# Tiles for the conditioning dot products asked for by POOL instead of SP, and other landing times in the plan of a two-layer gated trunk

## The chip, the core and the metric

The kernel runs on one core of one Trainium2 chip. The core has a tensor engine (PE, with PEld for its weight loads), a vector engine (DVE), a scalar engine (ACT), GpSimd (POOL) and SyncE (SP), which only issues transfers. Each engine takes its instructions in one fixed order; a DMA is issued by one of the engines (here SP or ACT), after the semaphores that it waits for, and runs beside them on the core's 16 DMA engines. The metric is the time of one execution in microseconds, the median of several; each comparison is with the kernel before.

## What is computed

Two layers over a residual stream of 512 tokens and 1024 features, float32. Cut to what matters:

```python
def hybrid_layer(x, c_silu, ...):
    mod = c_silu @ w_ada + b_ada
    shift, scale, gate = jnp.split(mod, 3, axis=-1)
    u = rms_norm(x, norm_g) * (1 + scale[:, None]) + shift[:, None]
    z = u @ w_in                      # queries, keys, values, gates of all mixers
    ...
    ya = dsa_attention(...) * jax.nn.silu(ag)      # mixer A: indexer, top-k, softmax
    yb = swa_sinks_attention(...) * jax.nn.silu(bg) # mixer B: window of 128, sinks
    yc = stick_breaking_attention(...) * jax.nn.silu(cg)  # mixer C
    merged = (jax.nn.sigmoid(ma) * (ya @ w_br_a) + jax.nn.sigmoid(mb) * (yb @ w_br_b)
              + jax.nn.sigmoid(mc) * (yc @ w_br_c))
    return x + gate[:, None] * (merged @ w_out)
```

The line `mod = ...` is the conditioning: 3072 dot products of length 1024 a layer. `c` is one vector, so there is no matrix to multiply with, and the kernel does these products on DVE.

## The kernel before

**Work and stages.** Features lie on partitions, tokens along the free axis, so a tile is 128 x 512. Each float32 weight tile is split into a high and a low part (`whi`, `wlo`), each activation too (`uh`, `ul`), and TensorE adds up three products of the parts. A layer goes through a first phase (seven column groups, accumulated over the features as they become ready), a value phase, a long body, and the output phase. In the body the mixers C, B and A follow one another, each in four steps of two heads, while the remaining columns of `w_in` and the branch matrices are multiplied in between. TensorE has such weight tiles to work on all through the body. The program's name for the tiles of `w_in` is in_w_t, in_w_v and in_w_first, for the branches in_w_br_a, in_w_br_b and in_w_br_c, for the output in_w_o.

**Weights on their way.** `Chunks` (line 728 ff.) takes all weight tiles in the order of use. `load` asks for a tile in one of four buffers `wstage`, by a DMA on SP; `do_split` makes `whi` (a cast, on ACT, DVE or POOL) and `wlo` (a subtraction, on DVE or POOL) out of it, four buffers of each. A sequence entry with the flag `is_raw` is not split: it is a tile for the dot products. `ada_g` gives such tiles of in_w_gt (the gate, 16 a layer, 32 in all) and `ada_ss` those of in_w_ss (shift and scale of layer 1, 32 tiles, asked for in the body of layer 0 only; layer 0's own shift and scale come through other buffers, `Y`, before). `dot` multiplies such a tile in place by the conditioning vector (`csr`) on DVE, with the sum in one instruction, and after every second tile adds the bias into `mods`. The raw tiles use the same four `wstage` buffers as the weights, in the order of the sequence. Layer 0's gate is first needed in the output phase, in_w_ss in the first phase of layer 1.

**Rotary shuffles and transposes.** `rope_evac` turns queries and keys: it copies the product into `zs`, and four DMAs on SP bring rows of `zs` into `m2` (m in the profile, 64 KB each). `softmax_tr32` transposes attention weights by 32 x 32 blocks on DVE and by 16 DMAs from `X` to `U` (or `V5`), issued by SP or ACT. TensorE's next queries and keys (`Q`, `KH`) wait for the first, the products with the values for the second.

**The order.** Nothing of the order is written by hand. `Recorder` records all instructions with their possible engines, a price for each (`price`), and their tiles; `order` runs `forward` five times, a list scheduler that plays the engines in time: each engine takes, of what it may do, what can start first, and among these the one with the earliest latest start (`latest`) of the round before. The best of the five orders is written out, and the chip's engines follow it, each its own list, with semaphores between them. The plan's times thus set the order on each engine, the engine of each cast and subtraction, and the buffer of each tile; the chip's own times set when things happen. For a DMA the plan books the issuing engine (`price`, "dma_start": 0.35 us on SP for a load from memory, 1.0 us on POOL) and gives a landing time (line 524 ff.), with a single channel, `dma_free`, on which transfers follow one another; `lag` is the size over 385 GB/s, in us: 0.68 for 256 KB, 0.48 for 182 KB, 0.21 for 80 KB, 0.17 for 64 KB. SP's time in the plan also stops when eight transfers are under way (`LANES`); transfers of all issuing engines count there.

Of the kernel before, what the change touches and what calls it, by code (L numbers as in the profile page):

```python
# [281 lines left out]
class Recorder:  # L282
# [149 lines left out]
    def forward(self):  # L432
        E = {e: {"free": 0.0, "port": 0.0, "mode": None, "ready": {}, "pend": []} for e in self.real}
        dma_free, lanes = 0.0, []
# [12 lines left out]
        def offer(x):  # L447
            if x.left == 0 and x.bound == 0:
                for e in x.alts:
                    heapq.heappush(E[e]["pend"], (max(x.est, x.soft.get(e, 0.0)), x.i))  # L450

        def give(c):
            while c.given < len(c.tiles) and c.free:
                t = c.tiles[c.given]
                c.given += 1
                if not t.users:
                    continue
                at, slot = heapq.heappop(c.free)
                t.slot, t.before, c.held[slot] = slot, c.held.get(slot), t
                for x in waiting[id(t)]:  # L460
                    x.est = max(x.est, at)
                    x.bound -= 1
                    offer(x)
# [7 lines left out]
        while len(out) < len(self.list):  # L471
            best = None
            for name, e in E.items():
                free, port, pend, ready = e["free"], e["port"], e["pend"], e["ready"]
                while pend and pend[0][0] <= free + 1e-9:
                    i = heapq.heappop(pend)[1]
                    ready[i] = self.list[i]
                mine = None
                for i in list(ready):
                    x = ready[i]  # L480
                    if x.taken:
                        del ready[i]
                        continue
                    y = x.alts[name]
                    at = max(free, port) if y.port else free
                    if len(x.alts) > 1 and self.elsewhere(x, name, at, E):
                        continue
                    key = (at, x.prio, i)
                    if mine is None or key < mine:
                        mine = key  # L490
                if mine is None or mine[0] > free + 1e-9:
                    while pend and self.list[pend[0][1]].taken:
                        heapq.heappop(pend)
                    if pend:
                        est, i = pend[0]
                        x = self.list[i]
                        at = max(est, port) if x.alts[name].port else est
                        key = (at, x.prio, i)
                        if (mine is None or key < mine) and not (len(x.alts) > 1 and self.elsewhere(x, name, at, E)):
                            mine = key  # L500
                        elif mine is None:
                            mine = None
                if mine is not None:
                    asked = max(free, self.list[mine[2]].est, self.list[mine[2]].soft.get(name, 0.0))
                    if best is None or (mine[0], asked, mine) < best[:3]:
                        best = (mine[0], asked, mine, name)
            assert best is not None, "no instruction may go"
            (at, _, i), name = best[2:]
            e, x = E[name], self.list[i]
            y = x.alts[name]  # L510
            x.taken, x.engine = True, name
            e["ready"].pop(i, None)
            hold = y.cost
            if name == "PE":
                if e["mode"] is not None and y.mode != e["mode"]:
                    hold += self.ENTER[y.mode]
                e["mode"] = y.mode
            x.start, x.hold = at, hold
            e["free"] = at + hold
            if y.port:  # L520
                E["POOL"]["port"] = at + y.lag + self.CROSS if name == "DVE" else at + hold
                E["DVE"]["port"] = at + y.lag - self.TOPORT
            if y.mode == "dma":
                if not x.writes:
                    x.end = at + 2.1
                else:
                    x.end = dma_free = max(at + (2.1 if at < 20.0 else 2.2 if y.lag < 0.22 else 3.0), dma_free) + y.lag * (1.2 if dma_free < 5.5 else 1.0)
                lanes.append(x.end)
                if name == "SP" and len(lanes) >= self.LANES:
                    e["free"] = max(e["free"], lanes[-self.LANES])  # L530
            else:
                x.end = at + y.lag + (hold - y.cost)
            out.append(x)
            for s in x.succs:
                s.est = max(s.est, x.end + self.between(x, s))
                s.left -= 1
                offer(s)
            for s in x.apart:
                for o in s.alts:
                    if o != name:  # L540
                        s.soft[o] = max(s.soft.get(o, 0.0), x.end + self.NEXT)
                s.left -= 1
                offer(s)
            for t in x.tiles:
                t.users -= 1
                t.done = max(t.done, x.end + self.CROSS)
                if t.users == 0:
                    heapq.heappush(t.pool.free, (t.done, t.slot))
                    give(t.pool)
# [99 lines left out]
def trunk(ctx, tc, xT, vecs, w_ss, w_gt, w_first, w_t, w_v, w_br, w_o, rope, consts, out):  # L649
# [8 lines left out]
    PE, ACT, DVE, POOL, SP = (rec.engine(e) for e in ("PE", "ACT", "DVE", "POOL", "SP"))  # L658
# [69 lines left out]
    class Chunks:  # L728
# [8 lines left out]
        def load(self, upto):  # L737
            while self.nload < min(upto + 1, len(self.seq)):
                i = self.nload
                if i >= 4 and i - 4 not in self.used:  # L740
                    break
                src, is_raw = self.seq[i][:2]
                n = src.shape[1]
                t = rec.tile("wstage", [P, S], F32)
                SP.dma_start(t[:, :n], src)
                self.raw[i] = (t, n)
                self.nload += 1

# [808 lines left out]
    def out_phase(l):  # L1557
# [57 lines left out]
        for d in range(KT - 2):  # L1615
            def fn(*ws, d=d):
                z, xr = zbank(), load(d)
                mms(d, ws, z, FULL)
                update(d, z, xr, FULL)
                save(d)  # L1620
            yield op(5200, fn, (w_o[l, d, 0], False), (w_o[l, d, 1], False))

        def tail(*ws):
            z, xr = [zbank(), zbank()], [load(6), load(7)]
            parts = HALVES if l + 1 < L else (slice(0, 256), slice(256, S))
            for cs_ in parts:
                for i in range(2):
                    mms(6 + i, ws[2 * i:2 * i + 2], z[i], cs_)
                    update(6 + i, z[i], xr[i], cs_)
                if cs_.start and l + 1 == L:  # L1630
                    last(parts[0])
                after(cs_)
            if l + 1 == L:
                last(parts[1])
            save(6)
            save(7)
            st["x"] = st["xn"]
            if l + 1 < L:
                st["xold"] = st["xsave"]
# [176 lines left out]
```

## Time and profile before

| | |
|---|---|
| median of 3 runs | 1138.33 us (1137.66 to 1138.64) |
| profiled execution | 1136.31 us |
| its span, first to last instruction | 1134.2 us |
| mean granted TensorE clock | 0.998 |
| TensorE's idle time in the span | 17.9 us |
| body of layer 0 / of layer 1, about | 108 to 570 us / 664 to 1122 us |
| mean rate of all DMA | 141 GB/s |

The profiled execution is 2.0 us below the median of the others. Matmul ends are modelled, so TensorE's busy time says that work was queued, not that it ran at its peak; its idle entries are real waits. In the page, L621 is the line of the helper that writes out all recorded instructions, so instructions are told apart by the tiles that they write and read (out<-in), not by their line. An engine's name with a q (SPq) is its sequencer, where DMAs are issued.

### The profile page before, as it was taken

Reading aid. Unit: us, or ns where it says so; the run is one execution under the profiler, and the core shown is the slowest. Engines: PE = TensorE matmul, PEld = TensorE weight load, DVE = VectorE, ACT = ScalarE, POOL = GpSimd, SP = SyncE. Lnnn points to the kernel's source line nnn. Section 1 sums busy time; section 2 is a strip of 40 time slices with the busy share of each in tenths; the row PEclk is TensorE's granted clock in tenths of the full one; section 3 lists DMA queues with packets and bytes.
Section 4 is the critical chain, followed back from the end, with each engine's and each line's share of the span. In section 5 each row is a group of like instructions: output and inputs, shape, how many; then the busy total and the mean of one; then the engine's idle time right before and its main releaser. Section 6 shows DMA issues by size and latency. Waiting matters only on the chain.

```text
span 1134.2 us, 17655 instructions
## 1 busy us (share of the span) xinstructions
PE 1116.3 (98%) x5579; PEld 926.8 (82%) x5579; DVE 900.4 (79%) x1966; ACT 615.8 (54%) x1298; POOL 254.0 (22%) x340
## 2 busy tenths in 40 slices
PE   8999999999999999999999999999999999999997
PEld 6899877788878787788898988777888878877886
DVE  7865999999989896677475479999998898666544
ACT  6644765863556563444365357757436466444343
POOL 1110344632113220010011004555421222101101
PEclk9999999999999999999999999999999999999999
DMA  9644334354465566455634342253545445524342
GB/s 341 240 123 129 94 94 127 107 146 152 125 170 154 160 199 179 134 151 177 183 111 111 101 137 84 76 157 105 156 131 145 143 140 149 150 83 148 94 130 102
DMA packets 94301, 159.86 MB, mean 141 GB/s; under 512 B 14592, under 2 KB 29184, under 8 KB 94208
## 3 DMA queue, kind: packets, MB, share of 16 engines
q1 hardware_dynamic: 86096, 146.25, 43.7%
q10 hardware_dynamic: 8112, 12.49, 3.9%
q8 instruction: 44, 0.72, 0.3%
q14 instruction: 49, 0.40, 0.1%
HBM read 125.39 MB, written 4.19 MB: 114 GB/s over the span
## 4 chain that ended last, share of the span: by engine, by line
PE 87%; DVE 4%; DMA 3%; POOL 2%; ACT 1%; issue 1%; SPq 1%; DVEq 0%; POOLq 0%; ACTq 0%
PE ps_z L621 68%; PE ps_s L621 15%; PE ps_s L619 3%; SPq L621 1%; PE ps_z L619 1%; DVE X L621 1%; DMA Y<-in_w_ss 1%; DVE wlo L621 1%; POOL wlo L621 1%; DMA m<-zs 1%; DMA U<-X 1%; POOL Q L621 1%; DMA wstage<-in_w_br_c 0%; DVE m L621 0%; DVE t L621 0%
## 5 line engine op out<-in xcount | busy, mean ns | idle before, releaser
L621 PE MATMUL ps_z<-uh,whi 128*128 128x512 f32 (+1 forms) x905 | 353.9, 392 | 2.1 <-ACT KH L621 1.9
L621 PE MATMUL ps_z<-ul,whi 128*128 128x512 f32 (+1 forms) x905 | 351.5, 389 | 0.0
L621 PE MATMUL ps_z<-uh,wlo 128*128 128x512 f32 (+1 forms) x905 | 351.1, 388 | 0.0
L621 DVE TENSOR_TENSOR wlo<-wstage,whi 128x512 fp32r<-128x512 f32 (+2 forms) x315 | 213.4, 680 | 118.5 <-ACT whi L621 99.4
L621 ACT CAST whi<-wstage 128x512 fp32r<-128x512 f32 (+2 forms) x226 | 133.8, 594 | 237.3 <-PE ps_z L621 142.3
L621 PEld LDWEIGHTS ps_z<-uh,whi 128*128 128x128 f32 x905 | 169.8, 188 | 38.4 <-ACT KH L621 2.3
L621 PEld LDWEIGHTS ps_z<-uh,wlo 128*128 128x128 f32 x905 | 169.8, 188 | 34.5 <-issue 0.2
L621 PEld LDWEIGHTS ps_z<-ul,whi 128*128 128x128 f32 x905 | 169.9, 188 | 33.1 <-issue 0.5
L621 POOL CAST whi<-wstage 128x512 fp32r<-128x512 f32 (+2 forms) x109 | 67.5, 619 | 489.2 <-PE ps_z L621 280.5
L621 PE MATMUL ps_z<-Y,whi 128*128 128x512 f32 x384 | 120.2, 391 | 0.2
L621 POOL TENSOR_TENSOR wlo<-wstage,whi 128x512 fp32r<-128x512 f32 (+1 forms) x57 | 73.2, 1286 | 90.8 <-DVE ul L621 56.8
L621 PEld LDWEIGHTS ps_z<-Y,whi 128*128 128x128 f32 x384 | 71.9, 188 | 16.0 <-ACT Y L621 1.1
L621 ACT ACTIVATE e<-e 128x512 f32<-128x512 f32 x96 | 59.6, 631 | 43.2 <-DVE e L621 41.7
L621 ACT ACTIVATE t<-t,nm 128x256 f32<-128x256 f32 (+3 forms) x128 | 65.3, 511 | 32.1 <-DVE nm L621 20.6
L621 PE MATMUL ps_z<-Y,wlo 128*128 128x512 f32 x192 | 74.8, 390 | 0.0
L621 ACT ACTIVATE t<-t 128x512 f32<-128x512 f32 x110 | 61.7, 631 | 7.3 <-POOL t L621 4.1
L621 DVE MAX8 m<-score 128x8 f32<-128x256 f32 (+2 forms) x96 | 53.2, 556 | 1.8
L621 ACT ACTIVATE e<-ps_z 128x512 f32<-128x512 f32 x68 | 40.2, 592 | 25.3 <-DMA V<-X 13.2
L621 DVE MATCH_REPLACE8 score<-m,score 128x256 f32<-128x256 f32 (+2 forms) x96 | 52.1, 543 | 0.0
L621 DVE STREAM_TRANSPOSE X<-X 128x640 f32<-128x640 f32 (+1 forms) x72 | 49.5, 729 | 1.7 <-ACT X L621 1.5
L621 PE MATMUL ps_s<-KH,Q 128*128 128x256 f32 (+3 forms) x280 | 48.5, 304 | 1.4 <-ACT KH L621 1.4
L621 DVE SCALAR_TENSOR_TENSOR wstage<-wstage,csr 128x512 f32<-128x512 f32 x64 | 45.0, 704 | 5.2 <-DMA wstage<-in_w_ss 5.1
(211 smaller groups left out, 1946.6 us busy)
## 6 DMA issues: line engine op xcount, KB each, us to landing
wstage<-in_w_t SPq DMA_DIRECT2D x212, 256.0 KB, 2.7
wstage<-in_w_v SPq DMA_DIRECT2D x48, 182.0 KB, 2.3
m<-zs SPq DMA_DIRECT2D x128, 64.0 KB, 2.2
wstage<-in_w_gt SPq DMA_DIRECT2D x32, 256.0 KB, 2.7
wstage<-in_w_ss SPq DMA_DIRECT2D x32, 256.0 KB, 2.9
wstage<-in_w_o SPq DMA_DIRECT2D x32, 256.0 KB, 2.7
Y<-in_w_ss SPq DMA_DIRECT2D x15, 512.0 KB, 6.2
wstage<-in_w_first SPq DMA_DIRECT2D x16, 256.0 KB, 4.0
```

Of the source, the lines that this page charges most:

```text
L619: self.real[engine].matmul(*[real(a) for a in q[:3]], start=q[3], stop=True, skip_group_check=True)
L621: made = getattr(self.real[engine], y.op)(*[real(a) for a in y.args], **{k: real(v) for k, v in y.kw.items()})
```

## The change

```diff
@@ in forward(), the landing of a DMA in the plan
                 if not x.writes:
                     x.end = at + 2.1
                 else:
-                    x.end = dma_free = max(at + (2.1 if at < 20.0 else 2.2 if y.lag < 0.22 else 3.0), dma_free) + y.lag * (1.2 if dma_free < 5.5 else 1.0)
+                    late, rate = (2.1, 1.2 if dma_free < 5.5 else 1.0) if at < 20.0 else (3.0, 1.0) if at < 60.0 else (2.3, 1.57) if y.lag > 0.4 else (2.0, 1.78) if y.lag > 0.19 else (2.2, 0.0)
+                    x.end = dma_free = max(at + late, dma_free) + y.lag * rate
                 lanes.append(x.end)
@@ in Chunks.load()
                 t = rec.tile("wstage", [P, S], F32)
-                SP.dma_start(t[:, :n], src)
+                (POOL if is_raw else SP).dma_start(t[:, :n], src)
                 self.raw[i] = (t, n)
```

Two things are edited. The 64 raw tiles (32 of in_w_gt, 32 of in_w_ss, 256 KB each) are asked for by POOL; all other loads stay with SP. And the plan's landing time is another: up to 20 us from the plan's start as before, from 20 to 60 us with a fixed part of 3.0 us for all sizes, and after that by three classes of size, each with a fixed part (2.3, 2.0, 2.2 us) and a factor on the size (1.57, 1.78, 0). Both enter the list scheduler, so the order of all engines is made anew. The amount of work, the buffers and the recorded sequence are the same.

## The prediction

> **What bounds the kernel now.** I read the page's busy times and chain first, then TensorE's waits, then the places of its idle time.
>
> ```profile
> span 1134.2 us, 17655 instructions
> PE 1116.3 (98%) x5579; PEld 926.8 (82%) x5579; DVE 900.4 (79%) x1966; ACT 615.8 (54%) x1298; POOL 254.0 (22%) x340
> PE 87%; DVE 4%; DMA 3%; POOL 2%; ACT 1%; issue 1%; SPq 1%; DVEq 0%; POOLq 0%; ACTq 0%
> ```
>
> TensorE is busy for all but 1134.2 - 1116.3 = 17.9 us of the span. The change takes no matmul away, so it can win only idle time, and lose by making new idle time. The next question is where those 17.9 us lie. In TensorE's waits (total, times, longest) these three rows are the ones that fall into the two layers' bodies; the others belong to the start, before 18 us, and to the end:
>
> ```profile
> PE ps_s L621 <- ACT t L621: 2.1, 2, 1.2
> ...
> PE ps_z L621 <- ACT KH L621: 1.9, 1, 1.9
> ...
> PE ps_s L621 <- ACT KH L621: 1.4, 1, 1.4
> ```
>
> The timeline of TensorE gives their places:
>
> ```profile
> 214.66 0.44 PE L621 MATMUL ps_s<-small,t 128*128 128x128 f32 x2 [0.86 <-ACT t L621]
> ...
> 334.17 0.50 PE L621 MATMUL ps_s<-KH,Q 128*128 128x512 f32 x1 [1.40 <-ACT KH L621]
> ...
> 379.88 0.47 PE L621 MATMUL ps_z<-uh,whi 128*128 128x512 f32 x1 [1.88 <-ACT KH L621]
> ...
> 771.02 0.44 PE L621 MATMUL ps_s<-small,t 128*128 128x128 f32 x2 [1.20 <-ACT t L621]
> ```
>
> That is 0.86 + 1.40 + 1.88 + 1.20 = 5.34 us, 0.47% of the time: **the most that this change can win**. The stall at 214.66 has its twin at 771.02, 556 us later, in layer 1: both belong to mixer C's last head pair. Those at 334.17 and 379.88 have no twin. The chain of waits shows that too, if the same two steps are compared in both layers:
>
> ```profile
> 282.92 3.18 PE ps_s L619 x32
> ...
> 448.49 4.46 PE ps_s L619 x32
> ...
> 839.26 3.18 PE ps_s L619 x32
> ...
> 1000.83 4.46 PE ps_s L619 x32
> ```
>
> Layer 0 takes 448.49 - 282.92 = 165.57 us from one to the other, layer 1 takes 1000.83 - 839.26 = 161.57 us. TensorE's work is the same; what layer 0 has beside it are the 32 tiles of in_w_ss for layer 1, with their dot products. So 4.00 us, of which 3.28 are the two idle times, go with in_w_ss.
>
> **Part 1, the loads leave SP.** The answers on the two tensors (min/median/max ns to issue, first and last start):
>
> ```profile
> L621 SPq DMA_DIRECT2D wstage<-in_w_ss x32: 327/328/1897, 305.3 to 520.0; - x32
> ...
> L621 SPq DMA_DIRECT2D wstage<-in_w_gt x32: 327/328/553, 92.2 to 855.7; - x32
> ```
>
> 64 issues leave SP's queue, mostly 0.33 us each: 64 x 0.33 = 21 us of SP's time, which ends nothing by itself. What counts is SP in the rush before 379.88. The chain there, and SP's timeline:
>
> ```profile
> 365.25 3.70 DMA U<-X
> 368.96 2.79 DMA U<-X
> ...
> 374.24 3.36 DMA m<-zs
> 377.60 0.03 issue
> ...
> 379.17 0.63 ACT KH L621
> ```
>
> ```profile
> 364.96 0.53 SPq L621 DMA_DIRECT2D wstage<-in_w_ss  x1
> 365.60 6.70 SPq L621 DMA_DIRECT2D U<-X  x8
> 372.39 2.43 SPq L621 DMA_DIRECT2D m<-zs  x4
> ```
>
> KH, for which TensorE waits, comes from the four row shuffles m<-zs; these stand in SP's queue behind eight transposes, and these behind one tile of in_w_ss, 0.64 us with the gap. Further, SP waits for landings of in_w_ss itself:
>
> ```profile
> SPq L621 <- DVE wlo L621: 325.1, 187, 7.1
> ...
> SPq L621 <- DVE wstage L621: 41.2, 33, 4.3
> ...
> SPq L621 <- DMA wstage<-in_w_ss: 2.3, 2, 1.2
> ```
>
> So the price of in_w_ss on SP at one stall is up to 0.64 + 1.2 = 1.8 us, about the 1.88 seen. Ahead of the other stall, the issue of 1.90 us (1897 ns, the longest of the 32) lies in the same queue; 1.90 - 0.33 = 1.57 covers the 1.40. Bounds for the relief: 0.64 us (one issue in one stall) and 4.00 us (the whole difference of the layers). I take the two idle times, **-3.3 us**, because the queue's own numbers come near each of them. What is late next once they go: the dot products stay on DVE, and m<-zs still needs its own four issues and a landing.
>
> The Trainium skill, page DMA: Bandwidth & Descriptors, section "Issuing engines are not separate DMA queues", speaks against this: DMAs of all issuing engines run on the same 16 DMA engines, and issuing from several saves only the issuer's time. By it alone the win would be the 0.64 us; the 1.2 us wait of SP for a landing, in the row above, is more than an issue, but whether it goes no run here shows yet. The rule is rival B below.
>
> **Part 2, the loads arrive on POOL.** No row shows a DMA issued by POOL. Below nothing is excluded, since a load gives POOL no result earlier. The nearest rows on both sides: SP issues the same transfer in 0.33 us, at the longest 1.90. POOL's own work on the same tile, and DVE's:
>
> ```profile
> L621 DVE TENSOR_TENSOR wlo<-wstage,whi x315: 523/682/1567, 14.5 to 1114.5; 128x512 fp32r<-128x512 f32 x129, 128x364 fp32r<-128x364 f32 x24, 128x384 fp32r<-128x384 f32 x5
> ...
> L621 POOL CAST whi<-wstage x109: 486/615/1114, 38.2 to 1083.8; 128x512 fp32r<-128x512 f32 x98, 128x364 fp32r<-128x364 f32 x10, 128x384 fp32r<-128x384 f32 x1
> ```
>
> I take 0.62 us, POOL's median instruction on this tile; the plan itself books 1.0 (its own constant). 64 of them are 40 us on an engine that is 78% idle. It hurts where POOL is on the path, and that is mixer C's last head pair:
>
> ```profile
> 185.00:224.00 39.00, 37.83 (x198) 29.03 (x197) 37.00 (x83) 23.46 (x44) 22.12 (x28) 1.00 0.50 143
> 224.00:305.00 81.00, 81.00 (x390) 66.90 (x390) 79.70 (x215) 42.81 (x112) 24.19 (x26) 1.00 0.44 130
> ```
>
> ```profile
> by line: POOL wlo L621 9.8%; issue 8.8%; SPq L621 8.3%; POOL Q L621 8.2%; DVE X L621 7.6%; DMA wstage<-in_w_br_c 7.4%; DVE wlo L621 7.3%; POOL whi L621 5.6%; DVE score L621 4.3%; DVE t L621 3.4%; DVE zc L621 3.3%; DVE G L621 3.3%; POOL zc L
> ```
>
> In the first 39 us (columns: PE, PEld, DVE, ACT, POOL busy) DVE is full, 37.00, and POOL, 22.12, carries 9.8 + 8.2 + 5.6 = 24% of the chain, a little more with zc. How many loads fall in it: in_w_gt has this row for 100 to 320 us,
>
> ```profile
> L621 SPq DMA_DIRECT2D wstage<-in_w_gt x14: 327/328/553, 102.5 to 299.4; - x14
> ```
>
> so one each (299.4 - 102.5)/13 = 15.1 us, 2.6 in 39 us. On the path: 2.6 x 0.62 x 0.27 = 0.4 us, in both layers **+0.9 us**. Lower end 0; upper end 2.6 x 1.90 = 4.9 us a layer, if each is of the longest kind and wholly on the path. Each load also brings a wait to POOL: for the wstage slot, one of four, whose last reader is usually DVE (the 325.1 and 41.2 us of SP's waits above, 1.7 and 1.2 us each). Behind it in POOL's order stand casts whi, and the KH, klow and Q pieces, for which TensorE waits. The plan places the load where it thinks the slot free, so I count nothing more for it here; its cost, if DVE runs late, is rival C.
>
> **Part 3, the landings in the plan.** It moves no byte; it alters where the list scheduler puts each instruction. By the two formulas, an undisturbed transfer after 60 us lands, in the plan, after 3.68 us before and 3.37 after (256 KB), 3.48 and 3.06 (182 KB), 2.41 and 2.38 (80 KB), 2.37 and 2.20 (64 KB). The trace:
>
> ```profile
> wstage<-in_w_t SPq DMA_DIRECT2D x212, 256.0 KB, 2.7
> wstage<-in_w_v SPq DMA_DIRECT2D x48, 182.0 KB, 2.3
> m<-zs SPq DMA_DIRECT2D x128, 64.0 KB, 2.2
> ...
> U<-X SPq DMA_DIRECT2D x46, 80.0 KB, 3.1
> ```
>
> All planned values come nearer to the medians, but for 80 KB, where 2.38 stays short of 3.1; there a queue of transfers counts, and eight of them now take 8 x 0.38 = 3.0 us of the plan's channel instead of 8 x 0.21 = 1.7. Splits of weights may go 0.3 us earlier, and the transposed U is expected later. Neither is on TensorE's path in steady stretches (the row for 224 to 305 us above, 81.00 of 81.00 us busy, is such a stretch). Any new list shifts which engine takes which cast, so stalls of the size seen, 0.9 to 1.9 us, can come or go. I take **0**, bounds -2.06 (the twin stalls 0.86 + 1.20 go) and +1.9 (one more stall of the largest size).
>
> **The sum.** -3.3 + 0.9 + 0 = -2.4 us against the profiled execution, 1136.31 us (span 1134.2, and 2.1 around it): 1133.9. The median of the shown runs, 1138.33, lies 2.0 above that execution; in its terms **1135.9 us**.
>
> **Rivals.**
> A. The forecast, relief on SP, own range 1133.3 to 1137.5: chance 0.42.
> B. The relief is hidden: the tiles of in_w_ss wait for their slot, not for SP (325.1 us of SP's waits are for DVE's wlo), and DVE's dots made layer 0 longer. For it: the m<-zs of the chain are mostly their own issue and landing. Then -0.64 + 0.9, and some shifting: 1138.6, within 0.2%. Chance 0.22.
> C. **POOL takes the wait over; slower.** Mechanism: in mixer C's last pair DVE and POOL keep each other out. The rows above have DVE's wlo at 0.68 us usually and 1.57 at the longest, 0.89 more, and POOL's cast 0.62 and 1.11. If a load on POOL meets this, it holds 0.62 + 0.89 = 1.5 us, and the chain there is about half POOL's and DVE's (24 and 29%): 2.6 x 1.5 x 0.53 = 2.1 us a layer, 4.2 in both; with a relief of only 1.0 us it gives +3.2: 1141.5. Against the full relief it turns the sign from 3.3 / (2 x 2.6 x 0.53) = 1.2 us for each load in that stretch. Against it: POOL is 78% idle, and the plan books 1.0. Chance 0.25, up to +8 us with the 1.90 end.
> The Trainium skill names such a thing: SBUF — State Buffer, the box on the "DVE blocks DMA" trap in "SBUF: two separate sides", says that a DMA issued by GpSimd has its descriptors written by GpSimd's cores, and that these are locked out while a DVE operation holds the shared port. The trace agrees as far as 1.57 us against 0.68 goes; no run here shows it for a DMA.
> D. The new list loses all four stalls: -5.3, 1133.0. For it: landings nearer to the trace. Against: the twins come from full DVE, which no landing changes. Chance 0.11.
>
> **Chances and range.** About 0.2% (2.3 us) is what a measurement of this kernel can tell from no change. Faster: 0.27 of A's 0.42, all of D's 0.11, 0.02 of B: 0.40. Slower: 0.23 of C, 0.03 of B: 0.26. Within: 0.15 + 0.17 + 0.02 = 0.34. A and B lie on both sides of the border, so the likeliest case's own range stands above; the range reaches from D's end, 1132.6, to 1142.6, somewhat beyond C.
>
> **What would show it.** Right: TensorE's idle entries near 334 and 380 gone or under 0.5 us, the two layers' stretch equal within 1 us, no wait of SP for in_w_ss. POOL's loads at 0.6 to 1.0 us each. Wrong: a load on POOL over 1.5 us, new idle of TensorE released by POOL's or DVE's wlo or KH, longer stalls at mixer C's last pair; or stalls of the same sum at other places, which would mean that the list and not SP sets them.

## The result, and the profile after

The change makes the kernel **slower**: 1148.32 us (median of 4 runs, 1147.16 to 1148.98) against 1138.20 (4 runs, 1137.66 to 1138.64), a ratio of 1.0088, 95% interval 1.0071 to 1.0106. The forecast was 1135.9, the range 1132.6 to 1142.6: the sign is wrong, and the time lies 5.7 us outside.

The head of the page after, with the queues, and the granted clock of the core:

```profile
span 1147.2 us, 17686 instructions
PE 1122.9 (98%) x5579; PEld 930.9 (81%) x5579; DVE 905.1 (79%) x1960; ACT 611.4 (53%) x1293; POOL 295.5 (26%) x415
...
PEclk9999999999999999999999999999999899999998
...
q0 software_dynamic: 5120, 16.78, 5.2%
```

```profile
core 0: 1147.2 us, clock 0.991
```

TensorE has the same 5579 instructions, but is busy for 6.6 us longer (1122.9 against 1116.3), and its mean clock is 0.991, 0.998 before: some matmuls ran slower. POOL has 41.5 us more work. The profiled execution took 1148.98 us, so its span of 1147.2 is to be set beside 1134.2: 13.0 us. (It is 0.7 us above its median, that of before 1.9 below its own, so the medians differ by 10.1.)

TensorE's waits in the bodies, the two largest entries of its timeline, and the windows around them (columns: PE, PEld, DVE, ACT, POOL busy, granted clock, DMA share, GB/s):

```profile
PE ps_s L622 <- ACT KH L622: 6.7, 2, 3.8
PE ps_z L620 <- DMA m<-zs: 1.1, 1, 1.1
```

```profile
341.45 1.22 PE L622 MATMUL ps_s<-KH,Q 128*128 128x512 f32 x3 [3.76 <-ACT KH L622]
...
343.43 0.63 PE L622 MATMUL ps_z<-uh,whi 128*128 128x512 f32 x1
343.86 0.63 PE L622 MATMUL ps_z<-ul,whi 128*128 128x512 f32 x1
...
351.20 0.40 PE L622 MATMUL ps_z<-uh,wlo 128*128 128x512 f32 x1
351.44 0.40 PE L622 MATMUL ps_z<-uh,whi 128*128 128x512 f32 x1
```

```profile
897.53 0.79 PE L622 MATMUL ps_s<-KH,Q 128*128 128x512 f32 x1 [2.97 <-ACT KH L622]
```

```profile
330.00:337.60 7.60, 7.60 (x34) 6.02 (x33) 7.51 (x18) 4.43 (x12) 1.15 (x2) 1.00 0.67 181
337.60:341.40 3.80, 0.09 (x1) 0.00 (x0) 2.87 (x7) 1.85 (x3) 0.00 (x0) 0.90 0.74 202
341.40:347.50 6.10, 6.05 (x17) 4.36 (x19) 3.61 (x8) 1.24 (x2) 3.05 (x3) 0.50 0.59 170
347.50:360.00 12.50, 12.50 (x79) 9.83 (x76) 11.50 (x21) 5.85 (x10) 5.50 (x6) 1.00 0.41 131
893.00:894.60 1.60, 1.56 (x7) 0.94 (x6) 1.50 (x3) 0.09 (x1) 0.00 (x0) 1.00 0.65 178
894.60:897.50 2.90, 0.00 (x0) 0.00 (x0) 2.87 (x7) 1.85 (x3) 0.00 (x0) 0.92 0.75 202
897.50:903.90 6.40, 6.37 (x16) 5.11 (x17) 3.80 (x6) 0.62 (x1) 1.01 (x2) 0.50 0.54 146
```

Both stalls are of one kind: the first score product of mixer A waits for its key KH, in layer 0 at 341.45 (the successor of the stall of 1.40 at 334.17) and in layer 1 at 897.53, where there was none. During each the granted clock falls, and it stays at **0.5** for 6.83 us. The matmuls behind a stall follow each other every 0.43 us (343.43, 343.86) instead of every 0.23 to 0.24 (351.20, 351.44). So a stall is followed by a second loss. The trace has 25 matmuls of 512 columns at half clock, which take 5.5 us more than at full clock; before there were none in the body.

The third loss is the end. POOL closes with a DRAIN record, for which all engines wait before they leave together; no view groups it, so its records stand here (us):

```
kernel                  loads on POOL   drain starts, takes, ends     SP's ends   span ends
before                        0        1128.88   1.51   1130.39       1133.48     1134.17
changed                      64        1139.65   6.77   1146.42       1144.24     1147.20
```

The last product of POOL is the same in both, 1.41 us long; behind it POOL drains for some 5 us more. From TensorE's last end (1127.46 and 1138.23) to the end of the span it is 6.71 us before and 8.97 after: 2.3 us.

**The accounts of 13.0 us**: TensorE's idle time after its start phase 6.5 to 10.5, +4.0; half clock +5.5; the end +2.3; the other 1.3 in matmuls of other shapes and at switches. The same by place, from the times at which TensorE has done the same number of matmul columns: +1.5 by 240 us, at mixer C's last pair of layer 0; +5.2 at the first key of layer 0; -2.3 near 380, where a stall went; +6.1 at the first key of layer 1; +0.3 elsewhere; +2.3 at the end.

### The profile page after: what moved, and what is told of

Read it like the earlier page. It is cut to its first block, busy times and chain, and to the rows that moved or that the text cites. A ratio compares the mean times of both kernels' runs of the same rounds, so it can differ in the third digit from the quotient of the medians.

```text
span 1147.2 us, 17686 instructions
## 1 busy us (share of the span) xinstructions
PE 1122.9 (98%) x5579; PEld 930.9 (81%) x5579; DVE 905.1 (79%) x1960; ACT 611.4 (53%) x1293; POOL 295.5 (26%) x415
## 4 chain that ended last, share of the span: by engine, by line
PE 83%; DVE 9%; DMA 3%; ACT 1%; issue 1%; SPq 1%; POOL 0%; ACTq 0%; DVEq 0%; POOLq 0%
PE ps_z L622 64%; PE ps_s L622 15%; PE ps_s L620 3%; DVE t L622 2%; DMA m<-zs 1%; PE ps_z L620 1%; DVE wlo L622 1%; SPq L622 1%; DVE m L622 1%; DVE score L622 1%; DMA U<-X 1%; DVE X L622 1%; DMA Y<-in_w_ss 1%; ACT t L622 1%; DVE e L622 1%
## 5 line engine op out<-in xcount | busy, mean ns | idle before, releaser
L622 DVE TENSOR_TENSOR wlo<-wstage,whi 128x512 fp32r<-128x512 f32 (+2 forms) x306 | 205.5, 674 | 115.5 <-ACT whi L622 98.7
L622 POOL TENSOR_TENSOR wlo<-wstage,whi 128x512 fp32r<-128x512 f32 (+1 forms) x66 | 84.5, 1284 | 110.0 <-DVE ul L622 56.7
L622 PEld LDWEIGHTS ps_s<-KH,Q 128*128 128x128 f32 x280 | 43.4, 193 | 14.5 <-ACT KH L622 7.6
L622 DVE MAX8 m<-score 128x8 f32<-128x384 f32 (+2 forms) x96 | 53.2, 556 | 1.4
L622 DVE MATCH_REPLACE8 score<-m,score 128x384 f32<-128x384 f32 (+2 forms) x96 | 52.1, 543 | 0.0
```

What stands on the lines that cost most here:

```text
L622: made = getattr(self.real[engine], y.op)(*[real(a) for a in y.args], **{k: real(v) for k, v in y.kw.items()})
```

## The experiments

"Before's list" is the order that the planner made for the kernel before. A kernel with another landing time, or with loads on POOL in the plan, gets another list. The expectations name theories by letters, and say in each what it holds. What two of them call the stalls at mixer B are those at the first key of mixer A. The kernel before ran again beside each set of experiments, with medians of 1135.53 to 1137.75 us, and each ratio is to those of its own set; times of different sets differ by as much. First the two edits apart, and the two lists crossed with the two engines.

**Landing times alone** (the new line of `forward`, loads on SP):

> Only the plan's landing times are new; all loads stay with SP. Theory L (the new landing times make the list that stalls TensorE at mixer B): 1146 to 1150 us, with TensorE idle by about 3 us there in both layers and the granted clock at 0.5 for some us behind each. Theory P (the loads on POOL do it, by their waits or their transfers): 1136 to 1140 us, no clock of 0.5 inside the body. Theory X (only the two together, any new list being a draw): between, with stalls at other places.

**Loads on POOL alone** (the new line of `load`, old landing times):

> Only the loads go to POOL; the plan keeps its old landing times, and makes a new list. Theory L: 1135 to 1140 us. Theory P: 1146 to 1150 us. Theory X: anything from 1135 to 1146 us, with stalls at other places than the changed kernel's.

**Before's list with the 64 loads issued by POOL, and the changed kernel's list with them issued by SP.** The same device in both, at the writing out of the order:

```diff
                 self.raw[i] = (t, n)
+                if is_raw:
+                    rec.moved.add(rec.list[-1].i)
...
                 y = x.alts[engine]
+                if x.i in self.moved:
+                    engine = "POOL"          # "SP" for the other
```

> The list of before to the letter; only the 64 raw loads are issued by POOL at the places at which SP issued them. No new plan, so this is the price of the move on the chip alone. Theory L: 1136 to 1139.5 us, the wait near 380 us shorter. Theory P: over 1142 us, with waits on POOL's loads in the chain.

> The list of the changed kernel to the letter; only the 64 raw loads are issued by SP again, at the same places. Theory L: 1146 to 1151 us, the two stalls at mixer B still there with the clock at 0.5 behind them. Theory P: 1138 to 1141 us, no stall over 2.5 us.

| kernel | list made for | loads on | ratio to before, 95% | POOL's drain, us |
|---|---|---|---|---|
| e1 | SP, new landings | SP | 1.0034, 1.0019 to 1.0048 | 1.51 |
| e2 | POOL, old landings | POOL | 1.0025, 1.0016 to 1.0035 | 6.76 |
| e3 | SP, old landings (before's) | POOL | 1.0086, 1.0069 to 1.0102 | 6.77 |
| e4 | POOL, new landings (the change's) | SP | 1.0044, 1.0027 to 1.0062 | 1.52 |
| the change | POOL, new landings | POOL | 1.0088, 1.0071 to 1.0106 | 6.77 |

No theory holds in all four. e3 comes out as P has it, at 0.86% (Theory L had 1139.5 us at most, 0.1%); e4 lies between L and P; e1 and e2 fit X best, as each costs about a third of the change.

e3 answers the main step of the prediction, since only the issuing engine differs from before. Its two entries at the places of 334.17 and 379.88:

```profile
337.32 0.50 PE L624 MATMUL ps_s<-KH,Q 128*128 128x512 f32 x1 [1.74 <-ACT KH L624]
```

```profile
384.57 0.77 PE L624 MATMUL ps_z<-uh,whi 128*128 128x512 f32 x1 [2.62 <-ACT KH L624]
```

```profile
374.69 0.10 DVE zc L624
...
376.84 0.59 SPq L624
377.43 0.04 issue
377.47 0.59 SPq L624
378.06 0.04 issue
378.11 4.17 DMA m<-zs
```

With no load of in_w_ss in SP's queue, 1.40 became 1.74 and 1.88 became 2.62. The last m<-zs of the chain (the fence shows the chain of waits; columns: start, length, what) now takes 4.17 us to land, 3.36 before. Each trace is one execution, and these lengths vary, but before's list was run in three more kernels below: e8 (nothing moved), e6 (one load, at 92 us, on POOL) and e16 (32 loads). The landing of that last m<-zs and the stall near 380 in all five (us):

```
kernel    loads on POOL    last m<-zs lands after    stall near 380
e6              1                  2.04                   0.51
e8              0                  3.11                   1.78
before          0                  3.36                   1.88
e3             64                  4.17                   2.62
e16            32                  5.15                   3.40
```

The rows of e6, where all 32 loads of in_w_ss are still in SP's queue, are these:

```profile
365.56 0.53 SPq L624 DMA_DIRECT2D wstage<-in_w_ss  x1
366.20 7.05 SPq L624 DMA_DIRECT2D U<-X  x8
373.35 2.44 SPq L624 DMA_DIRECT2D m<-zs  x4
...
379.53 0.47 PE L624 MATMUL ps_z<-uh,whi 128*128 128x512 f32 x1 [0.51 <-ACT KH L624]
```

The stall follows the landing of the row shuffle, with or without loads in the queue ahead of it. **The loads on SP were not what those stalls waited for.** Why that shuffle lands in 2.0 us once and in 5.2 another time, no run shows. e4, with the loads on SP, has waits of 0.40 and 0.31 us there.

Before, e8 and e3 have the same order on TensorE, so each matmul can be set beside itself. e8 stays within 1.2 us of before throughout. e3 loses 3.2 us from 185 to 217 us and 2.5 from 740 to 772, in mixer C's last head pair of the two layers, 2.8 from 360 to 390, 0.6 elsewhere, and 2.3 at the end. So in an unchanged list the move does cost most in the stretch that rival C named, though no load on POOL took over 0.78 us there.

e2 shows that a list can hide POOL's issues: TensorE ends at 1127.46, as before (the equal hundredths are luck: e8, before's list again, has 1127.84). What e2 loses is its end, 8.97 us behind the last matmul against 6.71.

e4 beside the changed kernel has the same order, with another issuer. ACT's timeline of e4, then of the changed kernel:

```profile
334.99 3.60 ACTq L625 DMA_DIRECT2D V<-X  x5
338.64 1.26 ACT L625 CAST KH<-zc 64x512 fp32r<-64x512 f32 x2 [4.12 <-DMA V<-X]
```

```profile
334.90 4.55 ACTq L622 DMA_DIRECT2D V<-X  x5
339.50 1.26 ACT L622 CAST KH<-zc 64x512 fp32r<-64x512 f32 x2 [5.07 <-DMA V<-X]
```

This list puts five transposes V<-X on ACT ahead of the casts of the key, and some wait for earlier landings. With loads on POOL they take 0.95 us longer, and the key starts 0.86 us later. DVE has the key's zc ready at the same time in both:

```profile
337.14 0.65 DVE L625 TENSOR_TENSOR zc<-zc,m 128x512 f32<-128x512 f32 x1
```

```profile
337.13 0.65 DVE L622 TENSOR_TENSOR zc<-zc,m 128x512 f32<-128x512 f32 x1
```

So of the 3.76 us in the change 1.72 (from 337.78 to 339.50) are ACT's wait for those landings, and the other 2.0 or so a key that is late by itself. TensorE's stall is 2.50 us in e4 and 3.76 in the change; in these two executions only the second is followed by half clock. In layer 1, too, the key is late by itself: ACT casts it as soon as zc is there.

**More small matmuls in the idle time**, to hold the clock up. The changed kernel, with 24 small products of a constant tile ahead of the first score product of each layer, and then with 10. They add work that nothing uses.

```diff
+                for group in first[:]:
+                    if x.i in group:
+                        first.remove(group)
+                        for _ in range(24):      # 10
+                            self.real[engine].matmul(real(y.args[0][:, :P]), real(self.fill), real(self.fill), start=True, stop=True, skip_group_check=True)
```

> The changed kernel's list; in each layer 24 small matmuls (about 2.6 us at the full clock; they add nothing to the result) run on TensorE just ahead of the first score matmul of mixer A, the one that waited 3.76 and 2.97 us. Theory K (the clock falls to 0.5 because TensorE idles about 3 us, and that is over half of the loss): no clock of 0.5 inside the body, 5 to 6.5 us faster than the changed kernel, that is a ratio to before of about 1.003 to 1.005. Rival (the clock falls for another reason, or costs little): as the changed kernel, ratio about 1.009, or slower by the matmuls added.

> The changed kernel with 10 (not 24) small products of a constant tile ahead of mixer A's first score product in each layer, so that TensorE never stands idle for the full 3.76 and 2.97 us; at the 0.213 us that each took in the kernel with 24, ten take 2.1 us a layer, inside the idle time. Theory C (the stalls cost as much again by the halved clock that follows them): the rows of clock 0.5 at 340 and 897 us go, some 5.5 us are won, 1142.5 to 1144, a ratio of 1.004 to 1.006 to the kernel before. Rival (the clock's rows are only a sign of the wait and give nothing back): 1147 to 1149, a ratio of 1.0085 or more.

With 24: 1146.54 us, 1.0090 (1.0055 to 1.0126). They took 0.21 us each, 5.1 a layer where the expectation had 2.6, so they filled more than the stalls. With 10: 1147.58 us, 1.0092 (1.0079 to 1.0106). In both the half clock in the body is gone, but neither kernel is faster than the change: theories K and C fail on the time, and the number is their rivals'. The timeline of the kernel with 10 shows why in layer 0:

```profile
340.49 0.74 PE L630 MATMUL ps_s<-KH,Q 128*128 128x512 f32 x3 [1.45 <-ACT KH L630]
...
351.02 0.50 PE L630 MATMUL ps_s<-KH,Q 128*128 128x384 f32 x2 [2.44 <-DVE e L630]
```

At full clock TensorE runs 3.2 us ahead of the changed kernel by 346, and then waits 2.44 us for DVE's e of the softmax, which the half clock had hidden. Just behind, at 352, it is 1.1 us ahead, as it was before the stall (0.9). In layer 1 the lead stays. In the profiled executions 3.0 us are left of it (span 1144.2 against 1147.2), in the medians nothing that can be told. So the 5.5 us in the accounts are what the half clock took, not what can be won back.

**The casts of the key on POOL instead of ACT**, in the changed kernel (`if x.i in self.keys and engine == "ACT": engine = "POOL"`):

> The changed kernel's list; the casts of mixer A's first key (KH) that the list has on ACT run on POOL, at the same places. Theory A (in layer 0 ACT's KH casts stand behind its transposes V<-X, which wait for earlier landings): the stall of 3.76 us of layer 0 shrinks by 1.5 to 1.8 us and its clock drop goes, the one of layer 1 stays, since its casts start as soon as zc is there: 3 to 5 us faster than the changed kernel. Rival (the key itself is late, by DVE's order and the row shuffles): no stall shorter by over 0.5 us.

1150.15 us, 1.0118 (1.0089 to 1.0147); the stall stays at 3.99 us. POOL starts the first cast 2.7 us earlier than ACT did, at 336.82, but its casts take longer, the last two 2.15 us where ACT needs 0.62 each. That is the rival's sign, but with slower casts it does not separate ACT's queue from a late key; the rows of zc above do.

**One load on POOL** (before's list with e3's device, `if is_raw and not rec.moved`, so only the first in_w_gt moved), and **32 of 64** (`len(rec.moved) < 32`, those issued up to 443 us):

> The list of before to the letter with a single load, the first tile of in_w_gt at 92 us, issued by POOL. Theory F (a fixed price: POOL's last drain takes 6.8 us in every run with loads on POOL, 1.5 us without, and all engines wait for it): 2.2 us slower than before, all of it after TensorE's last matmul. Rival (the drain grows with the number of loads, or its length is not on the path): less than 0.5 us slower.

> Before's list with the first 32 of the 64 loads (layer 0's) issued by POOL, the rest by SP. POOL's closing drain took 1.51 us with no load on POOL, 1.61 with one and 6.77 with 64, that is 0.08 us a load: with 32 an even growth gives 4.0 to 4.3 us, which ends about where SP's outputs have landed, so nothing or at most 0.2 us sticks out at the end. If only what was issued late counts: 1.5 to 2 us. One look; the body should carry about half of the 9 us of the kernel with all 64, all of it in layer 0.

With one load 1135.48 us, 0.9981 (0.9964 to 0.9997), drain 1.61 us. With 32 loads, in one execution, drain 4.15 us. With 0, 1, 32 and 64 loads on POOL the drain takes 1.51, 1.61, 4.15 and 6.77 us: it **grows evenly, 0.08 us a load**. With 32 it ends at 1141.76, before SP's at 1143.08, and sticks out no more. The second half of the expectation failed: the execution took 1146.07 us, about as long as with all 64, and TensorE ends 8.7 us late. The stall of 3.40 us at 384.97, again with 6.83 us at half clock, carries most of it. Theory F is refuted. That one moved load makes the kernel 0.2% faster is not shown: nothing in its trace explains it, and the medians of the kernel before differ by as much from set to set.

**POOL's last products to DVE**, in e2's kernel, so that the drain starts earlier (`if d in (...)` in `last` becomes `if False`):

> The kernel with the loads on POOL and the old landing times (1.0025 of before), with the five closing products that POOL had in the last update given to DVE, so that POOL's last work ends some microseconds earlier. Theory E (what that kernel loses is POOL's closing drain, 6.8 us long, which starts when POOL's own work is done and sticks out by 2.3 us): the drain starts 4 us or more earlier and is over before SP's; the time falls by 1 to 2.3 us less what DVE's five products add at the end (up to 2 us), a ratio of 0.9995 to 1.0015. Rival (the drain waits for the last work of the others, or for the outputs, and not for POOL's own): it still ends 2.3 us behind SP's, 1.0025 or more.

1138.28 us, 1.0013 (1.0001 to 1.0025). The drain runs from 1127.89 to 1133.98, SP's ends at 1136.32, and the end behind the last matmul is 6.77 us again. The mechanism holds; about half of the loss of e2 is back in the ratio, and these intervals overlap.

**Which landing time makes the worse list.** Before's kernel with the new values after 60 us only for a lag over 0.4 (the large transfers), and only for a lag up to 0.4:

> The kernel before, loads on SP, with the new landing time of the largest class alone (a lag over 0.4) after 60 us. If the large class's later landings make the worse list: near the 1.0034 of the kernel with all new landing times, with a stall of 1.5 us or more before the keys of mixer A. If the small classes make it: 0.999 to 1.001.

> The same with the new landing times of the small classes alone (a lag up to 0.4) after 60 us. If the large class makes the worse list: 0.999 to 1.001. If the small ones do: 1.003 or more. If both kernels are 1.002 to 1.004, no class carries it and any other list of the planner costs this much.

1141.12 and 1141.01 us, 1.0035 (1.0021 to 1.0048) and 1.0035 (1.0022 to 1.0047). Each half costs what the whole costs in e1. (Of the stalls expected, the small classes have one of 2.04 us before the first key of mixer A, the large class none over 1.5.) That fits no sum of two causes, so three lists were made with changes that have nothing to do with landings: the planner's `PIPE` at 0.18 and at 0.16 instead of 0.17, and 0.155 for 0.15 in VectorE's price. (0.171 gave before's own list: 1136.63 us, 0.9998, 0.9984 to 1.0012, a repeat of before and no test.)

> Neither half of the change: before with one constant of the plan, the latency of a matmul, at 0.171 in place of 0.170 us, only to have another list. Theory D (any new list is a draw whose spread is several us): a time 2 to 6 us off before's, more likely above, with stalls at other places. Theory L (the new landing times are to blame for the 0.34% of the run with landings only): within 1.5 us of before.

> The kernel before with the planner's PIPE at 0.18 us instead of 0.17: another list, but the loads stay on SP and the landing times stay old. Theory D (any list other than before's costs some 0.3%, as the planner's numbers are only near the chip's): 1.002 to 1.005, with stalls of 1 to 3 us at the keys of mixer A or the joins beside them. Rival (the new landing times themselves make the order worse): 0.999 to 1.001.

> The same with PIPE at 0.16 us. Theory D: 1.002 to 1.005. Rival: 0.999 to 1.001.

> The kernel before with 0.155 us instead of 0.15 in the planner's cost of VectorE's elementwise operations: another list, nothing about loads. Theory D: 1.002 to 1.005. Rival: 0.999 to 1.001.

0.9995 (0.9982 to 1.0008), 0.9988 (0.9978 to 0.9997) and 1.0029 (1.0015 to 1.0042). So lists of this planner differ by some 0.4% among themselves, for reasons that no edit aims at; that rests on three lists. That every other list is worse is refuted by two of the three; that the new landing times are worse in themselves is not shown, as one neutral edit costs nearly as much. It stays open. PIPE at 0.16 came out 0.1% below the kernel before, which is less than before's list with one load moved differs from before (0.9981), so no gain is shown; nothing better came up.

## Why the prediction was wrong

**What bounds the kernel.** The ceiling was right: only idle time could be won. The range then went 5.7 us below the kernel before and 4.3 above it, as if the stake were alike on both sides. The loss, 10.1, is not bounded by the idle time that there is. (The range's lower end, 1132.6, is called D's; D's own sum gives 1133.0. Nothing hangs on it.)

**Part 1, -3.3 us: failed.** The step "the queue's own numbers come near each of them" took agreement of sizes for a cause. In e3, where only the issuer differs, both stalls grow, and in e6 the one near 380 is 0.51 us with the loads still on SP: it goes by the landing of the last row shuffle. The issue of 1.90 us that was to cover the other stall began at 320.16, 12.6 us ahead of it. Nor was 1.88 a fixed size: before's list gave 0.51 and 1.78 in other executions. That SP's waits for in_w_ss went (no such row after) and that the two layers' stretch came to within 1.4 us (284.38 to 453.54 and 843.75 to 1011.51) looked like the forecast's signs (it asked for 1 us), but both stretches had become longer, 169.16 and 167.76 for 165.57 and 161.57.

**Part 2, +0.9 us: the price of a load was about right, what it costs was not.** 0.62 us a load was taken; the rows of the two tensors after (min/median/max ns, first and last start):

```profile
L622 POOL DMA_DIRECT2D wstage<-in_w_gt x32: 536/553/746, 92.5 to 861.7; - x32
L622 POOL DMA_DIRECT2D wstage<-in_w_ss x32: 536/538/586, 308.0 to 524.7; - x32
```

The sum counted mixer C's last pair, by POOL's time alone. In before's list (e3) that stretch loses 3.2 and 2.5 us, and 2.8 more go near 380, where the sum had nothing. It also stopped at the last load, at 862 us, and left out POOL's own close, 0.08 us for each of 64 loads, of which 2.3 us stick out: with e2, that is all that this part costs when the list suits it. In the list of the change it costs more. The ratios of the change and e4, 1.0088 and 1.0044, differ by 0.0044, 5.0 us, with some 2.8 either way by their intervals: 2.3 for the end, and the rest, as far as the two traces tell, for later keys and the half clock behind them. The two profiled executions lie 8.4 us apart.

**Part 3, 0: mis-sized.** The bound above was "one more stall of the largest size", +1.9. e4, the same list with SP, costs 5.0 us (0.0044 of 1138, 3.1 to 7.1 by the interval). In its profiled execution it is 4.6, of which 1.4 arise by 30 us (half clock behind a stall near 17 us, which before's list shows too, in e8) and 3.2 in the body: +0.5 by 240 us, +1.7 and +2.1 at the first keys of mixer A, -1.3 near 380, and little elsewhere. Two steps failed: a new list was priced by one stall of a size seen, while it loses at several places; and a stall was priced at its own length. The clock was left out: it stays whole in the body of e4's execution, but in the change it is halved for 6.83 us at each of the two stalls. The Trainium skill, TensorE: Matmul & The Clock Gate, section "Why this matters for your kernels", says to let TensorE stand idle for no more than some 3 us, or its clock halves; the stalls of 3.76 and 2.97 us agree, though in other runs here less was enough (last section). The prediction should have weighed that before it bounded a stall.

**Rivals.** B, the relief hidden anyway, was right about the relief; by itself it gave 1138.6. C had the sign, at a chance of 0.25, and in before's list the place: e3 loses there 3.2 and 2.5 us, where C had 2.1 a layer. Its mechanism is not borne out: no load on POOL took over 0.78 us in any run (0.75 in the change), where 1.5 was the price of its lock. In the list of the change mixer C's last pair has no stall over 0.8 us in layer 0. POOL's waits for the buffer did move to it, 115.3 us behind DVE's wlo, and e2 shows that a fitting list hides them:

```profile
POOL wstage L622 <- DVE wlo L622: 115.3, 31, 8.2
```

D is out: the stalls near 380 and 771 went and that at 215 shrank, but larger ones came at other places.

The mark "stalls of the same sum at other places, which would mean that the list and not SP sets them" was the right one to look for: the stalls came at other places, though of a larger sum, and e4 shows the list alone making part of them. The chances gave it too little.

## What to carry to other kernels

When an edit lets a planner make a new order, price the order and not the edit: a few neutral changes of the planner's numbers show how far its lists differ (here 0.4%), and an edit worth less than that can't be judged by one list. Swap the issuer in an unchanged list before you call a queue the cause of a stall, and profile the same list more than once: a number of the right size is no cause, and a stall of 1.88 us can be 0.51 the next time. Bound a stall of the tensor engine above by its length and the half clock behind it, and look past the last matmul for what an engine must still close.

## What the runs showed that was not expected

- **The clock goes by windows, not by the length of a stall.** In each trace all starts of half clock lie whole multiples of 3.413 us apart: in the changed kernel 340.67, 897.04 and 1139.39, that is 163.0 and 71.0 of them. Each piece of half clock in the body lasts 3.41 or 6.83 us, one or two of them. The Trainium skill, TensorE: Matmul & The Clock Gate, section "Part 1: The HAM clock gate", names a free-running window of 3413 ns; the length of the pieces agrees with it, and so does their grid.
- **A little over half a window of idle time is enough.** If that grid is carried through each of the 18 traces, from 8 us to the last matmul, and TensorE's idle time is added up in each window, then every window with 1.80 us of it or more (18 windows, 53% and up) is followed by half clock, and none with 1.71 us or less (50%) is. So it is the sum in a window that counts: 0.90 and 1.18 us in one window halved the clock (e11, at 768.73), and so did 1.91 us (e3, at 199.69), while the stall of 2.50 in e4, cut by a border of the grid, left 1.69 us in a window and did not. By these figures a lone stall under 1.7 us doesn't halve the clock, one over 3.6 us always does, and in between it is luck where it falls. Why some pieces last two windows the traces don't settle.
- A stall of 1.9 us near 17 us, in the start phase, is in all 18 traces, and in 7 of them is followed by 3.41 us at half clock, also in one of two traces of the same list (before and e8): these 7 are among the 18 windows. It adds to the spread of one kernel's runs.
- **POOL's close grows with the DMAs that it issued**, 0.08 us each, though the last of them was issued 280 us earlier. Why, no trace here shows.
- DMAs from POOL landed in 3.0 and 3.1 us (in_w_gt, in_w_ss), 2.7 and 2.9 from SP.
